# Float32 gathers from the residual, sums in other places, and a router without dependence on the group

## The chip, the cores and the metric

The kernel runs on one NeuronCore of a Trainium2 chip. The metric is the device time of one execution in microseconds, as the median of several runs. The engines are TensorE (PE; its weight loads are shown apart as PEld), VectorE (DVE), ScalarE (ACT), GpSimd (POOL) and SyncE (SP), whose queue issues nearly all the loads from HBM.

## The reference, cut to what matters

One decoder block on 256 tokens of width 2048, all in float32: two token mixers side by side, an output projection with a residual add, and a mixture of 32 experts. The change concerns the residual add and what follows it.

```python
x = x + mixed @ w_out[l]
x = x + hierarchical_moe(rms_norm(x, norm_ffn_g[l]), ...)
return rms_norm(x, norm_final_g)

def hierarchical_moe(h, ...):           # 4 groups of 8 experts, d_expert = 512
    group_prob = softmax(ht @ wr_group + br_group)
    g_prob, g_idx = top_k(group_prob, 1)
    expert_logits = (ht @ wr_expert + br_expert).reshape(n_tok, 4, 8)
    sel = expert_logits[arange(n_tok), g_idx[:, 0]]
    top_logit, top_idx = top_k(sel, 2)
    weights = softmax(top_logit) * g_prob
    gates = sum(one_hot(g_idx * 8 + top_idx, 32) * weights[..., None], axis=1)
    for e in range(32):
        hid = silu(ht @ w_gate[e]) * (ht @ w_up[e])
        out = out + gates[:, e:e + 1] * (hid @ w_down[e])
```

## The kernel before

**Dense part** (0 to about 798 us). The input projection, both mixers and their output projections run in an order that a list scheduler in the kernel works out at build time. Weights come as halves of 512 KB (`wr`, line 333, on SyncE's queue); ScalarE casts a half to `wh`, VectorE subtracts to get `wl`, and three matmuls (hi x hi, hi x lo, lo x hi) stand for one float32 product. The last step there makes the merged branches `mix` (16 steps j, four buffers). Then a loop written by hand does the output projection: four blocks n of 512 columns, eight steps kh each, and behind each block `after(n, pss)`: VectorE adds the block to the residual `acc`, ScalarE sums squares, TensorE transposes, ScalarE copies to `xT`, TensorE adds the router's logits into `pl`, and `xn` gets the block's split into a high and a low part (the function `split`: a cast on ScalarE, a subtraction on VectorE). The residual x is loaded into `acc` (line 1236) and the router's weights into `rt` (line 1244) from GpSimd's queue.

**Buffers.** Everything large lives in slots of [128, 2048] float32 (8 KB a partition) handed out by `slot(name)`; `room(n)` says whether n are left, `free(n)` gives back n. The `Experts` object `xw` streams the experts' weights: 384 tiles of 1 MB in one fixed order, for each expert eight gate/up tiles (`mgu`), and with one expert's delay four down tiles (`md`). A tile goes into a slot (`wt`) or into one of NX = 4 buffers `wx` that exist only after the dense part's pools are closed. `xw.issue` issues as many as there is room for (line 301, SyncE's queue), `xw.done` gives the used buffer back and issues the next.

**Router and experts.** After block 3 the root of the mean square (`rr`) scales the logits (`lg`); `first_max` finds the group, then the best and second-best expert in it, on 16 elements a partition; `asg` marks the chosen experts, four matmuls with a triangular mask count the tokens (`pos`, one less than the count), and `weights()` makes the gates. `gather(b)` builds, for the eight experts of group b, the compact inputs `xg`: a one-hot `oh` from `pos`, and for each of eight steps (d2) matmuls with lhsT = a part of `xn` (high and low) and the one-hot as moving operand, then two scaled copies on ScalarE. `spread(q)` makes one-hots `ohr`, gates and the transposed one-hots `ogT` for four experts. In the loop over e, expert 0's gather runs a step at a time between its own gate/up matmuls (`gu`); for later groups the gather runs beside the experts before (`beside`). Each expert: eight gate/up steps, `hd` = silu(gate) x up (ScalarE, VectorE), transposes, four down steps of the expert before (`down`), and `scatter`, which adds into `acc` two half experts at a time. `store` normalises and writes the output.

The profile names nearly all engine operations by the helper's line 167, so that tiles tell them apart.

## Time and profile before

| what | us |
| --- | --- |
| median of 3 runs | 1789.11 (1785.33 to 1793.22) |
| the profiled execution | 1787.91 |
| its span, first to last instruction | 1786.14 |
| TensorE matmuls busy | 1451.9 (81%) |
| VectorE busy | 821.4 (46%) |
| ScalarE busy | 556.5 (31%) |
| read from HBM | 526.82 MB |

The span counts from the first to the last instruction; what lies around it is 1.8 us. A timeline row is a run of like instructions: start, length, engine, line, operation, out<-in, shape, count; in brackets the idle time before it and the instruction that ended it. In a row of windows PEclk is the clock that TensorE was granted (1.00 is 2.4 GHz, 0.50 is 1.2 GHz), and the DMA share is the mean over 16 engines.

### The profile page before, as it was taken

What the parts mean: (1) busy time and instruction counts of PE and PEld (TensorE: products, weight loads), DVE (VectorE), ACT (ScalarE), POOL (GpSimd) and SP (SyncE); (2) the same over time, 40 slices, a digit from 0 to 9 for tenths busy, and PEclk for the clock granted to TensorE, in tenths of its full rate; (3) what the DMA queues carried; (4) which work ended last, traced back from release to release, by engine and by line L of the source; (5) the groups of instructions that cost most, each with busy time, mean ns of one, the idle gap of its engine ahead of it and who ended that gap; (6) DMA issues with size and microseconds to landing.
All of it is one profiled execution on the core that took longest, in us unless ns stands there. A gap on an engine that the chain in (4) does not pass through costs nothing.

```text
span 1786.1 us, 29643 instructions
## 1 busy us (share of the span) xinstructions
PE 1451.9 (81%) x12604; PEld 960.8 (54%) x12604; DVE 821.4 (46%) x1241; ACT 556.5 (31%) x919; POOL 33.6 (2%) x64
## 2 busy tenths in 40 slices
PE   7999999999999999996767776667676776676673
PEld 6989998888988999874323222223121332221120
DVE  6999998889944567442212121212121212121213
ACT  6668556666555344442001000011000110000002
POOL 0000000000100000000000000000000000000000
PEclk9999999999999999997978777798877888777766
DMA  6554463334635478538999999999999999999993
GB/s 232 180 163 133 147 209 107 118 105 158 190 117 177 152 254 331 176 125 330 414 421 421 420 421 421 421 420 421 421 421 421 421 420 421 421 421 420 420 421 149
DMA packets 94953, 534.09 MB, mean 299 GB/s; under 512 B 10528, under 2 KB 10544, under 8 KB 45024
## 3 DMA queue, kind: packets, MB, share of 16 engines
q1 hardware_dynamic: 91792, 522.49, 74.5%
q0 software_dynamic: 3024, 9.64, 1.8%
q8 instruction: 102, 1.67, 0.4%
q14 instruction: 35, 0.29, 0.0%
HBM read 526.82 MB, written 5.28 MB: 298 GB/s over the span
## 4 chain that ended last, share of the span: by engine, by line
DMA 49%; PE 40%; DVE 5%; ACT 3%; issue 2%; SPq 0%; DVEq 0%; ACTq 0%
PE mm L167 23%; DMA wt<-in_mgu_dram 21%; DMA wt<-in_md_dram 12%; DMA wx<-in_mgu_dram 11%; PE s L167 7%; PE sd L167 6%; DMA wx<-in_md_dram 3%; PE gu L167 2%; DVE wl L167 2%; DVE vring L167 1%; PE tr L167 1%; ACT wh L167 1%; PE y L167 1%; DMA x<-in_x_dram 1%; ACT ring L167 1%
## 5 line engine op out<-in xcount | busy, mean ns | idle before, releaser
L167 PE MATMUL mm<-hT,wh 128*128 128x256 f32 x2144 | 397.4, 287 | 5.7 <-ACT sg L167 3.0
L167 PEld LDWEIGHTS mm<-hT,wh 128*128 128x128 f32 x2144 | 330.1, 189 | 21.2 <-issue 9.9
L167 PE MATMUL gu<-wt,xg 128*32 128x256 f32 x2896 | 236.8, 457 | 102.8 <-DMA wt<-in_mgu_dram 94.5
L167 DVE TENSOR_TENSOR wl<-wr,wh 128x1024 fp32r<-128x1024 f32 x213 | 259.1, 1217 | 123.2 <-ACT wh L167 121.4
L167 PE MATMUL mm<-hT,wl 128*128 128x256 f32 x1072 | 302.7, 282 | 0.9 <-DVE wl L167 0.9
L167 ACT CAST wh<-wr 128x1024 fp32r<-128x1024 f32 x213 | 222.2, 1043 | 236.3 <-PE mm L167 150.2
L167 PEld LDWEIGHTS gu<-wt,xg 128*32 128x32 f32 x2896 | 88.8, 125 | 223.6 <-DMA wt<-in_mgu_dram 143.0
L167 PEld LDWEIGHTS mm<-hT,wl 128*128 128x128 f32 x1072 | 202.8, 189 | 1.5 <-DVE wl L167 1.3
L167 DVE TENSOR_TENSOR acc<-acc,sc 128x1024 f32<-128x1024 f32 x128 | 150.5, 1217 | 93.2 <-PE sc L167 93.2
L167 DVE SCALAR_TENSOR_TENSOR hd<-gu,gs,hd 64x256 f32<-64x256 f32 x32 | 15.7, 491 | 320.1 <-ACT hd L167 269.0
L167 DVE SCALAR_TENSOR_TENSOR ys<-y,gs,ys 128x512 fp32r<-128x512 f32 x32 | 24.0, 751 | 272.0 <-ACT ys L167 272.0
L167 PE MATMUL gu<-wx,xg 128*32 128x256 f32 x1200 | 104.7, 482 | 45.6 <-DMA wx<-in_mgu_dram 45.0
L167 ACT ACTIVATE ys<-y,gs 128x512 fp32r<-128x512 f32 x32 | 22.0, 687 | 280.0 <-PE y L167 280.0
L167 ACT ACTIVATE hd<-gu,gs 64x256 f32<-64x256 f32 x32 | 15.0, 468 | 259.5 <-PE gu L167 259.1
L167 PEld LDWEIGHTS gu<-wx,xg 128*32 128x32 f32 x1200 | 37.9, 130 | 99.5 <-DMA wx<-in_mgu_dram 68.7
L167 PE MATMUL sc<-ys,ogT 32*128 32x512 f32 x512 | 55.5, 509 | 28.8 <-DVE acc L167 27.7
L167 ACT ACTIVATE xg<-tr,prm 128x256 f32<-128x256 f32 x64 | 26.9, 471 | 161.2 <-PE tr L167 145.2
L167 ACT CAST ogT<-tr 128x256 fp32r<-128x256 f32 x32 | 11.8, 373 | 160.8 <-PE tr L167 160.7
L167 PEld LDWEIGHTS sc<-ys,ogT 32*128 32x128 f32 x512 | 23.6, 213 | 63.6 <-issue 43.6
L167 PEld LDWEIGHTS tr<-oh,xn 128*128 128x128 f32 x256 | 36.0, 209 | 15.5 <-issue 14.4
L167 PE MATMUL tr<-oh,xn 128*128 128x256 f32 x256 | 42.9, 315 | 1.0 <-DVE oh L167 1.0
L167 DVE TENSOR_TENSOR vring<-s,ring 128x512 f32<-128x512 f32 x64 | 42.4, 683 | 0.1
(462 smaller groups left out, 2042.4 us busy)
## 6 DMA issues: line engine op xcount, KB each, us to landing
wt<-in_mgu_dram SPq DMA_DIRECT2D x181, 1024.0 KB, 19.8
wt<-in_md_dram SPq DMA_DIRECT2D x87, 1024.0 KB, 19.8
wx<-in_mgu_dram SPq DMA_DIRECT2D x75, 1024.0 KB, 19.8
wr<-in_win_dram SPq DMA_DIRECT2D x132, 512.0 KB, 3.6
wx<-in_md_dram SPq DMA_DIRECT2D x41, 1024.0 KB, 19.8
wr<-in_wglu_dram SPq DMA_DIRECT2D x32, 512.0 KB, 3.8
wr<-in_wout_dram SPq DMA_DIRECT2D x32, 512.0 KB, 4.3
wr<-in_wro_dram SPq DMA_DIRECT2D x16, 512.0 KB, 6.7
```

The lines of the kernel that those rows point to most:

```text
L167: return self._tl.do(Op(self._k, lambda: f(*a, **k), c, outs, ins, own, fn, name == "dma_start"))
```

## The change

It has several parts that go together.

- The residual is now called `res`, and the gathers read it directly: lhsT is a float32 part of `res` and the one-hot is float32, so that four float32 matmuls stand where eight matmuls on the split parts stood. The split `xn` and its four slots go.
- The sums `acc` are two other slots, filled from `res` by four copies on ScalarE at the end of expert 0.
- The four buffers of `mix` are cut by k and given back in parts during block 3 (two at kh = 3, one at 5, one at 7); tiles are issued during `mix` up to 8 (before 7) and in the output projection when there is room.
- The best and second-best expert are found for all four groups at once, beside the group's own choice; `pos` keeps its one, and the one-hots compare with 1 to CAP. The Sqrt and the Silu table are loaded early by activations on a constant. Six matmuls whose result nobody reads stand between the logits and the choice.
- The gather runs one step ahead of the gate/up matmuls; `spread(0)` is cut in three, and its transposes come after `hd`.
- The branch for a group with too many tokens (not run with these inputs) is adapted.

```diff
-    acc = [slot("acc").rearrange("p (i c) -> p i c", i=2) for _ in range(2)]
+    res = [slot("res").rearrange("p (i c) -> p i c", i=2) for _ in range(2)]
...
-    xn = [[slot("xn", F32R) for _ in range(2)] for _ in range(2)]
     rt = slot("rt")
...
+        if n == 3:
+            act.activation(cst[:, 5:6], cst[:, 0:1], AF.Sqrt)
         for i in range(2):
-            a = A(i, n * 512)
+            a = B(i, n * 512)
...
         for i in range(2):
-            act.copy(xT[i], pts[i])
+            if n == 3 and i == 0:
+                dve.tensor_copy(xT[i], pts[i])
+            else:
+                act.copy(xT[i], pts[i])
...
-        for i in range(2):
-            cs = slice(n * 512, (n + 1) * 512)
-            split(xn[i][0][:, cs], xn[i][1][:, cs], A(i, n * 512))
...
-            if kh % 3 == 2:
+            if kh % 3 == 2 and (n < 3 or kh < 3):
                 xw.issue(xw.n + 1)
...
+            if n == 3 and kh in (3, 5, 7):
+                free(2 if kh == 3 else 1)
+                if kh == 3:
+                    xw.issue(xw.n + 1)
...
-    free(4)
+    ps = psd()
+    for _ in range(6):
+        pe.matmul(ps[:, :T], lhsT=ident, rhs=iot, start=True, stop=True)
...
+    acc = [slot("acc").rearrange("p (i c) -> p i c", i=2) for _ in range(2)]
     xw.more = NX
...
+    dve.tensor_reduce(m1, l32, axis=AX.X, op=OP.max)
+    dve.tensor_reduce(gm, l4, axis=AX.X, op=OP.max)
+    dve.tensor_tensor(x1, l32, e8(m1), op=OP.is_lt)
+    dve.tensor_tensor(xg_, l4, bc(gm, 4), op=OP.is_lt)
...
-    dve.tensor_scalar(pos, pos, 1.0, None, op0=OP.subtract)
...
+        act.activation(cst[:, 5:6], cst[:, 0:1], AF.Silu)
...
-                    for x_ in range(2):
-                        pe.matmul(ps[:, dd * 256:(dd + 1) * 256], lhsT=xn[i][x_][:, d * 128:(d + 1) * 128],
-                                  rhs=oh[i].rearrange("p a b -> p (a b)"), start=(i + x_ == 0), stop=(i + x_ == 2))
+                    pe.matmul(ps[:, dd * 256:(dd + 1) * 256], lhsT=B(i, d * 128, 128),
+                              rhs=oh[i].rearrange("p a b -> p (a b)"), start=(i == 0), stop=(i == 1))
...
-    next(gq)
+    for _ in range(2):
+        next(gq)
     ov2 = weights()
+    sp0 = spread(0)
+    next(sp0)
...
-                    next(gq)
+                    next(gq, None)
...
-                for _ in gq:
-                    pass
-                for _ in spread(0):
-                    pass
+                next(sp0)
                 gq = beside(0)
...
             act.copy(hT_, hps[:, 0:128])
+            if e == 0:
+                for h in range(2):
+                    for i in range(2):
+                        act.copy(acc[h][:, i], res[h][:, i])
```

What stands on SyncE's queue at the end of the dense part, before (`wr` are the last halves of the output projection's weights, `wx` and `wt` tiles of experts):

```order
L333 DMA wr_8609<-in_wout_dram 128x2x512
L333 DMA wr_8637<-in_wout_dram 128x2x512
L301 DMA wx_8769<-in_mgu_dram 128x2048
L301 DMA wx_8771<-in_mgu_dram 128x2048
L301 DMA wx_8773<-in_mgu_dram 128x2048
L301 DMA wx_8775<-in_mgu_dram 128x2048
L301 DMA wt_8777<-in_mgu_dram 128x2048
L301 DMA wt_8779<-in_mgu_dram 128x2048
L301 DMA wt_8781<-in_mgu_dram 128x2048
L301 DMA wt_8890<-in_mgu_dram 128x2048
L301 DMA wt_8911<-in_mgu_dram 128x2048
```

And after:

```order
L333 DMA wr_8607<-in_wout_dram 128x2x512
L333 DMA wr_8635<-in_wout_dram 128x2x512
L301 DMA wt_8655<-in_mgu_dram 128x2048
L301 DMA wx_8771<-in_mgu_dram 128x2048
L301 DMA wx_8773<-in_mgu_dram 128x2048
L301 DMA wx_8775<-in_mgu_dram 128x2048
L301 DMA wx_8777<-in_mgu_dram 128x2048
L301 DMA wt_8888<-in_md_dram 128x2048
L301 DMA wt_8905<-in_md_dram 128x2048
L301 DMA wt_8922<-in_md_dram 128x2048
L301 DMA wt_8939<-in_md_dram 128x2048
```

Before, seven tiles stand ahead of the first `wx`; after, twelve, the last of them behind the last half of the weights, and the four down tiles of expert 0 follow the `wx` directly. The first issue that waits for a tile of expert 1 is number 22 of the tiles before and number 24 after (counted from 0).

TensorE at the first gather, before (`tr` is the gather's result, `gu` the gate/up product of expert 0, `oh` the one-hots):

```order
L167 MATMUL tr_8871<-oh_686_8843,xn_8068 128x256
L167 MATMUL tr_8871<-oh_686_8843,xn_8069 128x256
L167 MATMUL tr_8871<-oh_687_8844,xn_8070 128x256
L167 MATMUL tr_8871<-oh_687_8844,xn_8071 128x256
L167 MATMUL gu_8870<-wt_7497,xg_8841 32x256 x8
L167 MATMUL tr_8892<-oh_686_8843,xn_8068 128x256
L167 MATMUL tr_8892<-oh_686_8843,xn_8069 128x256
```

And after:

```order
L167 MATMUL tr_8833<-oh_682_8829,res_8068 128x256
L167 MATMUL tr_8833<-oh_683_8830,res_8068 128x256
L167 MATMUL tr_8873<-oh_682_8829,res_8068 128x256
L167 MATMUL tr_8873<-oh_683_8830,res_8068 128x256
L167 MATMUL tr_8873<-oh_682_8829,res_8068 128x256
L167 MATMUL tr_8873<-oh_683_8830,res_8068 128x256
L167 MATMUL gu_8872<-wt_7499,xg_8827 32x256 x8
L167 MATMUL tr_8890<-oh_682_8829,res_8068 128x256
```

The second gather (`tr_8873`) now stands ahead of the first gate/up matmuls, the moving operand is the same one-hot, and the weights come from `res` instead of the two parts of `xn`.

ScalarE from the last block to the first gather, before (`rr` is the root, `ro_ge` and `ro_e` exponentials of the router):

```order
L167 ACTIVATE rt_8072,ssp<-acc_8065 128x512 x2
L167 COPY rt_8072<-sd_8729 128x512
L167 COPY rt_8072<-sd_8734 128x512
L167 ACT_TABLE_LOAD
L167 ACTIVATE rr<-rr,cst 128x2
L167 CAST xn_8068<-acc_8065 128x512
L167 CAST xn_8070<-acc_8065 128x512
L167 ACT_TABLE_LOAD
L167 ACTIVATE ro_ge_8794<-ro_ge_8794 128x8
L167 ACTIVATE ro_e_676_8821<-ro_e_676_8821 128x2
L167 CAST identr_8838<-ident 128x128
L167 ACTIVATE xg_8841<-tr_8871,prm 128x256 x2
```

And after:

```order
L167 ACT_TABLE_LOAD
L167 ACTIVATE cst<-cst 128x1
L167 ACTIVATE rt_8072,ssp<-res_8069 128x512 x2
L167 COPY rt_8072<-sd_8731 128x512
L167 ACTIVATE rr<-rr,cst 128x2
L167 ACT_TABLE_LOAD
L167 ACTIVATE ro_ge_8804<-ro_ge_8804 128x8
L167 CAST identr_8824<-ident 128x128
L167 ACTIVATE xg_8827<-tr_8833,prm 128x256 x2
L167 ACTIVATE ro_e_686_8841<-ro_e_686_8841 128x2
L167 ACT_TABLE_LOAD
L167 ACTIVATE cst<-cst 128x1
```

The first table load now stands ahead of the last block's squares, one of the two copies to `rt` and the two casts to `xn` are gone, and a third table load stands after the first gather's copies. Further down, `hd` of expert 0 stands directly behind the last `xg`; before, four casts to `ogT` and a table load stood between.

## Rows read from the trace of the kernel before

**Rows 1.** Windows: stretch, length, busy time (count) of each engine, PEclk, DMA share, GB/s.

```profile
690.00:798.00 108.00, 108.00 (x549) 90.97 (x548) 55.22 (x63) 47.19 (x64) 0.00 (x0) 1.00 0.52 172
...
804.00:818.00 14.00, 7.48 (x38) 5.51 (x38) 8.34 (x44) 2.09 (x7) 0.55 (x1) 0.51 1.01 424
...
842.00:846.00 4.00, 3.03 (x30) 1.54 (x34) 1.78 (x3) 0.66 (x2) 0.00 (x0) 0.50 0.00 0
...
880.00:1757.00 877.00, 608.48 (x5516) 217.97 (x5516) 184.32 (x202) 70.86 (x165) 1.01 (x2) 0.78 1.01 418
```

**Rows 2.** Chain of waits, start and length in us, the pieces that are tile transfers.

```profile
859.55 20.37 DMA wt<-in_mgu_dram
...
1727.72 19.82 DMA wx<-in_md_dram
```

**Rows 3.** Timeline of SyncE's queue: start, length, engine, line, operation, out<-in, count.

```profile
845.37 3.74 SPq L301 DMA_DIRECT2D wx<-in_mgu_dram  x3
```

**Rows 4.** Timeline of TensorE's matmuls, 808 to 844 us; idle time before in brackets.

```profile
808.54 0.61 PE L167 MATMUL tr<-ro_asg,mask 128*128 128x32 f32 x2 [6.31 <-DVE ro_asg L167]
...
811.01 2.07 PE L167 MATMUL tr<-oh,xn 128*128 128x256 f32 x8 [1.01 <-DVE oh L167]
814.00 1.94 PE L167 MATMUL gu<-wt,xg 128*32 128x256 f32 x16 [0.92 <-ACT xg L167]
...
819.51 1.21 PE L167 MATMUL tr<-oh,xn 128*128 128x256 f32 x8
821.28 1.07 PE L167 MATMUL gu<-wt,xg 128*32 128x256 f32 x16 [0.56 <-ACT xg L167]
...
836.15 1.95 PE L167 MATMUL tr<-ro_gtr,ohr 128*128 128x2 f32 x16
837.96 2.24 PE L167 MATMUL tr<-identr,ohr 128*128 128x128 f32 x8
...
843.38 5.34 PE L167 MATMUL gu<-wx,xg 128*32 128x256 f32 x48
```

**Rows 5.** Timeline of ScalarE, 800 to 842 us.

```profile
800.71 1.28 ACT L167 ACT_TABLE_LOAD   x1
802.00 0.30 ACT L167 ACTIVATE rr<-rr,cst 128x2 f32<-128x2 f32 x1
...
840.63 1.28 ACT L167 ACT_TABLE_LOAD   x1
```

**Rows 6.** Timeline of VectorE, 802 to 811 us.

```profile
802.93 1.28 DVE L167 TENSOR_TENSOR xn<-acc,xn 128x512 fp32r<-128x512 f32 x2
804.13 0.15 DVE L167 TENSOR_REDUCE ro_gm<-lg 128x2 f32<-128x8 f32 x1
...
805.38 0.27 DVE L167 TENSOR_REDUCE ro_sel<-ro_selp 128x16 f32<-128x64 f32 x1
...
808.17 0.22 DVE L167 TENSOR_TENSOR ro_asg<-ro_ohs,ro_go 128x64 f32<-128x64 f32 x1
...
810.30 0.20 DVE L167 TENSOR_SCALAR ro_pos<-ro_pos 128x64 f32<-128x64 f32 x1
```

**Rows 7.** Timeline of TensorE, two places with float32 matmuls of 256 columns.

```profile
195.13 1.10 PE L167 MATMUL sd<-SA,rkb 128*128 128x256 f32 x4 [0.21 <-ACT sg L167]
195.88 0.59 PE L167 MATMUL mm<-hT,wh 128*128 128x256 f32 x2
...
356.05 1.32 PE L167 MATMUL sd<-xg,gu 128*128 128x256 f32 x4
357.31 0.50 PE L167 MATMUL mm<-hT,wh 128*128 128x256 f32 x2
```

**Rows 8.** Weight loads of two tiles, duration min/median/max in ns.

```profile
L167 PEld LDWEIGHTS sd<-SA,rkb x4: 186/190/190, 195.1 to 195.6; 128*128 128x128 f32 x4
...
L167 PEld LDWEIGHTS tr<-oh,xn x192: 186/188/338, 921.6 to 1458.0; 128*128 128x128 f32 x192
```

**Rows 9.** DMA issues, 640 to 870 us: form, queue, count, KB, median us to landing.

```profile
rt<-in_rw_dram POOLq DMA_DIRECT2D x1, 288.0 KB, 12.7
```

More of the change, by code (lines that the diff above doesn't have):

```diff
@@ L411, in hybrid_block @@
     pool.iota(iot, pattern=[[1, T]], base=0, channel_multiplier=0, allow_small_or_imprecise_dtypes=True)
+    io8 = cp.tile([128, 8, 8], F32, name="io8")
+    pool.iota(io8, pattern=[[0, 8], [1, 8]], base=0, channel_multiplier=0, allow_small_or_imprecise_dtypes=True)
     mask = cp.tile([128, 2, 128], F32, name="mask")
@@ L1179, in front @@
             yield "wait"
-        mh = [[slot("mix", F32R) for _ in range(2)] for _ in range(2)]
-        St["mix"] = lambda k: [t[k // 8][:, (k % 8) * T:(k % 8 + 1) * T] for t in mh]
+        mh = [slot("mix", F32R) for _ in range(4)]
+        St["mix"] = lambda k: [mh[k // 4][:, (k % 4 * 2 + x_) * T:(k % 4 * 2 + x_ + 1) * T] for x_ in range(2)]
         yk = [[t[:, k * T:(k + 1) * T] for t in Y] for k in range(8)]
@@ L1191, in front @@
             if j % 2:
-                ctl(lambda: xw.issue(min(xw.n + 1, 7)))
+                ctl(lambda: xw.issue(min(xw.n + 1, 8)))
             while out_[0] > 1:
@@ L1232, in hybrid_block, with B @@
     mix = St["mix"]
[L1234 removed]
+    res = [slot("res").rearrange("p (i c) -> p i c", i=2) for _ in range(2)]
     for h in range(2):
[L1236 removed]
+        nc.gpsimd.dma_start(res[h], x.rearrange("(i p) c -> p i c", i=2)[:, :, h * 1024:(h + 1) * 1024])
+    def B(i, c, w=512):
+        return res[c // 1024][:, i, c % 1024:c % 1024 + w]
     def A(i, c, w=512):
         return acc[c // 1024][:, i, c % 1024:c % 1024 + w]
[L1241 removed]
     rt = slot("rt")
@@ L1377, in weights @@
     def weights():
+        e4, e2 = R("e4", [4]), R("e2", [1])
+        dve.tensor_sub(e4, m2, m1)
+        dve.tensor_mul(e4, e4, goh)
+        dve.tensor_reduce(e2, e4, axis=AX.X, op=OP.add)
+        act.activation(e2, e2, AF.Exp)
+        act.activation(cst[:, 5:6], cst[:, 0:1], AF.Silu)
         gs = R("gs", [1])
@@ L1388, in weights @@
         dve.tensor_mul(w2, w1, e2)
-        dve.tensor_mul(oh1, oh1, bc(w1, 8))
-        dve.tensor_mul(oh2, oh2, bc(w2, 8))
+        o8 = lambda o: o.rearrange("p i g e -> p i (g e)")
+        dve.tensor_mul(o8(oh1), o8(oh1), bc(w1, 32))
+        dve.tensor_mul(o8(oh2), o8(oh2), bc(w2, 32))
         dve.tensor_add(oh1, oh1, oh2)
-        dve.tensor_mul(gts.rearrange("p i (g e) -> p i g e", g=4), bc(oh1[:, :, None, :], 4, 8), g48)
+        dve.tensor_mul(gts.rearrange("p i (g e) -> p i g e", g=4), oh1, e8(goh))
         dve.tensor_copy(gtr[:, :, :, 0], gts)
         dve.tensor_copy(gtr[:, :, :, 1], bc(rr, 32))
-        ovf = R("ovf", [32])
-        dve.scalar_tensor_tensor(ovf, pos, float(CAP), gts, op0=OP.is_ge, op1=OP.mult)
-        ov1 = R("ov1", [32])
-        dve.tensor_scalar(ov1, pos, float(CAP), None, op0=OP.is_ge)
+        ovf, ov1 = (x_.rearrange("p i g e -> p i (g e)") for x_ in (x1, x2))
+        dve.scalar_tensor_tensor(ovf, pos, float(CAP + 1), gts, op0=OP.is_ge, op1=OP.mult)
+        dve.tensor_scalar(ov1, pos, float(CAP + 1), None, op0=OP.is_ge)
         ov2 = stile([128, 1], "ov2", 1)
@@ L1415, in gather @@
         xg = [slot("xg") for _ in range(2)]
-        oh = [stile([128, 8, CAP], "oh%d" % i, 1, F32R) for i in range(2)]
+        oh = [stile([128, 8, CAP], "oh%d" % i, 1) for i in range(2)]
         for i in range(2):
             pb = pos[:, i, 8 * b:8 * b + 8][:, :, None].to_broadcast([128, 8, CAP])
-            dve.tensor_tensor(oh[i], iot[:, None, 0:CAP].to_broadcast([128, 8, CAP]), pb, op=OP.is_equal)
+            dve.tensor_tensor(oh[i], iot[:, None, 1:CAP + 1].to_broadcast([128, 8, CAP]), pb, op=OP.is_equal)
         G8[b] = xg
@@ L1605, in hybrid_block @@
             down(e - 1, hT_)
+        else:
+            for _ in sp0:
+                pass
         if e < NE:
@@ L1624, in hybrid_block @@
             for i in range(2):
-                for x_ in range(2):
-                    pe.matmul(ps[:, i * 128:(i + 1) * 128], lhsT=xn[i][x_].bitcast(F32)[:, d * 128:(d + 1) * 128],
-                              rhs=dg[:, i], start=(x_ == 0), stop=(x_ == 1))
+                pe.matmul(ps[:, i * 128:(i + 1) * 128], lhsT=B(i, d * 128, 128), rhs=dg[:, i], start=True, stop=True)
             act.activation(h2[d // 8][:, (d % 8) * 256:(d % 8 + 1) * 256], ps[:, :256], AF.Copy, scale=P("ffng", d))
```

52 lines of the change are left out of this document (23 added, 29 removed).

## The prediction

> **What bounds the kernel now.** I read the windows by stage first, then the chain of waits, then the queue that issues the loads, then TensorE around the start of the experts. From 880 to 1757 us the DMA engines are busy all the time at 418 GB/s while TensorE works 608 of 877 us [rows 1]: the expert stage is bound by the 384 tiles of 1 MB. The chain says the same: from 859.55 us on it consists of tile transfers of some 20 us, each released by one that landed [rows 2]. By the count of issues the tile issued at 859.55 is number 33 (from 0) and landed at 879.92; the one that landed at 1747.54 is number 379 [rows 2]. That is 867.62 us for 346 tiles, 2.51 us a tile, without a gap. So the end is fixed by when the unbroken stream begins and with which tile. Just before it there is a hole: between 842 and 846 nothing moves at all [rows 1]. At 845.37 tile 22 is issued, in the buffer that expert 1's first tile gave back [rows 3]; expert 1's matmuls had begun at 843.38 [rows 4]. Of the tiles, 7 are in before the end of the dense stage, and 22 (0 to 21) are in or under way without expert 1. So: **end = issue of the first tile that waits for expert 1, plus 2.51 us for each tile left, plus a tail that the diff doesn't touch.** Two things can move it: that tile's number, and expert 1's start. Loading earlier by itself is worth nothing, since the hole would only open sooner.
>
> **Two buffers more.** Before, two buffers hold the sums and four the split of x; after, two hold x and two the sums. Two tiles more fit, and the issue order shows the first that waits for expert 1 at number 24 instead of 22. 2 x 2.51 = **5.0 us gained**. The sums take their buffers only after the eighth gate/up tile of expert 0, so nothing in front of it waits for them. Their four copies of 128x1024 on ScalarE run beside expert 1's matmuls, with about 7 us until ScalarE's next use: nothing. If that cover is gone, they cost some 4 us once. The five tiles more that load in the dense stage cost nothing if the weights' stream keeps its pace (a rival, below).
>
> **Router.** Removed from the path: the square-root table, 1.28 us before the root at 802.00 [rows 5], now loaded under the last block. But the logits also wait for the router's matmuls; with one of the two copies moved to VectorE these end some 0.5 us earlier, so of 1.28 us I take 0.9. The last split of x, two subtractions of 1.28 us together, lies between the logits and the first maximum at 804.13 [rows 6]: its part there is 1.1 us. The choice itself takes 804.13 to 808.39 [rows 6]. After, 13 steps depend on each other, on 64 elements; the nearest row of that size in such a chain is 0.27 us [rows 6], 3.5 us, and five small ones in between at about 0.1 make 3.5 to 4.0; saved 0.3 to 0.7, I take 0.5. The subtraction of one goes: 0.26 [rows 6]. Sum 0.9 + 1.1 + 0.5 + 0.3 = **2.8 us** (2.3 to 3.2). The six dummy matmuls lie in the gap of 6.31 us in which TensorE waits for the choice [rows 4]; at the size of [rows 7] their twelve instructions take 2.3 to 3.8 us, so they delay nobody. The Trainium skill, page "ScalarE: Activation LUTs", section "What ACT_TABLE_LOAD costs", counts 2.66 us for every switch, load and drain; here the root starts 0.01 us after a load of 1.28 [rows 5], so no drain shows. By the page the two loads taken off the path would bring 2.8 us more, a time of 1775.9.
>
> **Expert 0.** From the first gather to the end of its eight steps it takes 836.15 - 811.01 = 25.1 us [rows 4]. In the regular part a step is 2.77: gather 1.21, 0.56 of waiting for ScalarE's xg, gate/up 1.0 [rows 4]. One step ahead, the wait of 0.56 goes. The gather becomes four float32 matmuls, which run as eight instructions. Of that kind two rows are there [rows 7]: four in 0.75 us, from 195.13 to the next start at 195.88, which makes 1.5 us for eight; and four in 1.26 us (356.05 to the next start), 2.5 us for eight. In the gather, as in the first, the next matmuls come straight behind, and the last of the four overlaps them; I take 1.73, nearer to the first. A step is 1.73 + 1.0 = 2.73, eight are 21.9, with a first fill 22.1: 3.0 us less. Against it stands the clock: it was 0.51 from 804 to 818 [rows 1], after TensorE had had little to do since 802, and the first gather and the first gate/up took 2.07 and 1.94 instead of 1.21 and 1.07 [rows 4]. Before, about 7 us of gathering passed until the clock was back. At the low level the step takes double, so it loses half of what passes: 0 to 4.4 us. The dummies shorten the idle time and gathering begins without the pause of 0.92 [rows 4], so I take 2.6 lost, net **0.4 us gained** (3.0 gained to 1.4 lost; with the first row's 1.5 a step, 1.8 more gained).
>
> **From expert 0 to expert 1.** 836.15 to 843.38 are 7.23 us [rows 4]. In them: 1.95 for the gates' small matmuls, 2.24 for the transposes of the one-hots [rows 4], ScalarE's four casts behind them, the Silu table at 840.63 for 1.28 [rows 5], ScalarE's and VectorE's hd of 0.5 each, then two transposes. After, the table is loaded during expert 0, and hd stands ahead of the casts, right after the gates; the transposes run beside it. 1.95 + 2.24 + 0.47 = 4.7; and since the casts now come behind hd, the last pair of transposes may wait for a buffer, up to 0.9. So 4.6 to 5.5, I take 5.0: **2.2 us gained** (1.7 to 2.6). What is late next there is TensorE itself.
>
> **Later gathers.** The other three gathers have 0.5 us more work in each of eight steps (1.73 against 1.21), 4 us in some 56. TensorE is idle 30% of the stage [rows 1], so it is hidden.
>
> **Sum.** 5.0 + 2.8 + 0.4 + 2.2 = 10.4 us; ends 5.0 + 2.3 - 1.4 + 1.7 = 7.6 and 5.0 + 3.2 + 3.0 + 1.8 + 2.6 = 15.6. The profiled execution (1787.91, span 1786.14) would become 1777.5. It lies 1.2 under the median of 1789.11, so the forecast is 1778.7.
>
> **Rivals.** *The clock stays high* (0.22): the dummies hold it through the choice. Then nothing is lost in expert 0: 13.0 gained, 1776.1. Against it: what remains of the gap is some 4 us, and the dummies leave up to 2 of it empty.
> *Float32 gathers at the upper row* (0.13): 2.52 a step, 6.3 us more in eight steps; 4.1 gained, 1785.0. For it: [rows 7]'s second row, against it the first. The Trainium skill, page "TensorE: Matmul & The Clock Gate", section "Weight-path perf modes — Fast Weight Load (FWL) and DoubleRow", says that the fast load of 128 weights is given only where the type is not FP32, which speaks for it. The two load rows show 190 ns for float32 and 188 for the split kind [rows 8], so the trace shows no such difference.
> *The dense stage stalls* (0.15): the order puts both 1 MB loads of x after the late mix steps and the router's weights behind the last branch matmul (near 701 us), and VectorE's scaling of these stands in its queue ahead of subtractions that TensorE needs; five more tiles share the queue with the weights. TensorE is never idle from 690 to 798 [rows 1], so every stall there counts in full. The router's weights took 12.7 us to land [rows 9]; landing at 713.7 they would hold the subtractions up, which TensorE needs near 709.4, and with 2 us of scaling and subtracting the stall is 6.3; if they land in 5 us it is nothing. Taking 4: 6.4 gained, 1782.7.
> *The clock stays low through expert 0* (0.05), **the slower side**: each step is 3.46 + 1.94 = 5.4, eight are 43.2 against 25.1, and 5.0 + 2.8 + 2.2 no longer cover the 18.1: 8.1 lost, 1797.2. It decides from an expert 0 of 35.1 us. Against it: the clock came back in 7 us of the same sort of work before.
> *It doesn't do what it says* (0.05): the two tiles more are not under way because something else fills the buffers; 5.4 gained, 1783.7.
>
> **How the numbers follow.** The forecast itself has 0.40, with 1775.3 to 1781.5 of its own. A measurement of this kernel can tell about 0.5%, 8.9 us, from no change, a bound at 1780.2. Above it lie the float32 rival, the stall, the missing buffers and a part of the forecast; below it, most of the forecast and the high clock. Faster: 0.22 + three quarters of 0.40 + a little of the stall = 0.56. Slower: the low clock and a long stall, 0.07. The rest, 0.37, is within. The range goes from the sum's upper end (1773.5, with the clock kept and the shorter gather) to the upper float32 row with a bit over, 1773 to 1786; what it leaves out is the low clock, a long stall and the scatter of a median.
>
> **What would show it.** Right: twelve tiles issued before the wx tiles; tile 24 issued near 840 and expert 1 starting near 838; the end of the dense stage still at 798.2; a gather step of four float32 matmuls near 1.7 us at full clock; 4.6 to 5.5 us between expert 0's last gate/up and expert 1's first; a DMA hole longer than before, from about 830 to 840; the last tiles 10 us earlier. Wrong: TensorE idle between 700 and 720 (the stall), clock near 0.5 up to 830 (slower side), a step of 2.5 at full clock, or a hole after expert 1 has begun, in which case the stream isn't unbroken and the two tiles don't count.

## The result

| | kernel before | changed kernel |
| --- | --- | --- |
| median of 7 runs, us | 1789.11 (1785.33 to 1795.61) | 1779.18 (1774.03 to 1781.03) |
| the profiled execution, us | 1787.91 | 1781.03 |
| its span, us | 1786.14 | 1779.26 |
| first wx issue, us from the start | 798.22 | 804.93 |
| from the first wx issue to the end of the span, us | 987.9 | 974.3 |

The ratio is 0.9931, with a 95% interval of 0.9916 to 0.9947: faster, by 9.5 to 15 us. The forecast was 1778.7. The first wx issue, the first of the four tiles that go into the wx buffers, marks the end of the dense part. The two spans differ by only 6.9 us, and the last two lines of the table say why: behind that mark 13.6 us were gained, ahead of it 6.7 were lost. These are two separate findings.

**What was lost lies in code that the change doesn't touch.** Windows of the changed kernel around 355 us (stretch, length, busy time and count of PE, PEld, DVE, ACT, POOL, then the granted clock, the DMA share and GB/s):

```profile
350.00:355.00 5.00, 4.62 (x49) 2.73 (x47) 3.25 (x4) 4.55 (x9) 0.00 (x0) 1.00 0.31 105
355.00:360.00 5.00, 4.89 (x19) 3.77 (x19) 2.71 (x7) 0.90 (x2) 0.00 (x0) 0.69 0.31 108
360.00:365.00 5.00, 5.00 (x17) 3.58 (x16) 2.47 (x5) 1.21 (x2) 0.00 (x0) 0.50 0.00 0
```

And three windows of the kernel before, at the same place of the program:

```profile
350.00:355.00 5.00, 4.86 (x51) 2.80 (x49) 3.25 (x4) 4.56 (x9) 0.00 (x0) 1.00 0.32 105
355.00:360.00 5.00, 4.64 (x23) 3.04 (x23) 3.89 (x10) 1.61 (x5) 0.00 (x0) 1.00 0.32 108
360.00:365.00 5.00, 5.00 (x30) 3.73 (x30) 3.96 (x8) 3.89 (x5) 0.00 (x0) 1.00 0.00 0
```

The clock (the third number from the end) is 0.50 in one and 1.00 in the other, and TensorE gets 17 matmuls through in five microseconds instead of 30. This code is the same in both kernels. In the records of the weights' stream the changed kernel is 0.6 us ahead at 350 us and 6.8 us behind at 374, and stays at 6.6 until the output projection begins. Not every execution falls into this: the seven times of the changed kernel lie at 1774.0 to 1775.6 (three) and 1779.2 to 1781.0 (four), and of the twelve profiled executions here that have no edit in that place (before, changed and ten of the experiments) three show the low clock near 357 us. All three are of the changed kernel or its variants, ten of the twelve; the two on the kernel before are too few to say whether it falls there as often. An experiment below goes after it.

**What was gained.** The same stretches as in [rows 1] for the changed kernel; the program is 6.7 us later here, so read 842 to 846 against 835 to 839 of the kernel before:

```profile
690.00:798.00 108.00, 108.00 (x577) 92.11 (x576) 55.50 (x65) 47.12 (x62) 1.14 (x2) 1.00 0.71 253
...
842.00:846.00 4.00, 3.96 (x32) 2.28 (x36) 1.29 (x2) 3.31 (x7) 0.00 (x0) 0.50 0.01 4
```

TensorE is busy for the whole of 690 to 798, so the stall that I feared in the dense part isn't there, though the loads carry 253 GB/s where they carried 172. The hole in the loads is there as before (0.01 of the DMA engines at 842 to 846); it begins sooner, since tile 23 has landed at 840.6. SyncE's queue (start, length, engine, line, operation, out<-in, count):

```profile
786.99 0.34 SPq L301 DMA_DIRECT2D wt<-in_mgu_dram  x1
804.93 1.99 SPq L301 DMA_DIRECT2D wx<-in_mgu_dram  x4
...
845.42 0.33 SPq L301 DMA_DIRECT2D wt<-in_mgu_dram  x1
```

The issue at 845.42 is tile 24, the first to wait for expert 1. Counted from the first wx issue this is 40.5 us, where [rows 3] has tile 22 at 47.2. TensorE around expert 0, to be read against [rows 4]:

```profile
808.31 2.84 PE L167 MATMUL sd<-iot,ident 128*128 128x256 f32 x12
812.42 0.38 PE L167 MATMUL tr<-ro_asg,mask 128*128 128x32 f32 x2 [1.28 <-DVE ro_asg L167]
...
814.02 5.41 PE L167 MATMUL tr<-oh,res 128*128 128x256 f32 x16 [0.77 <-DVE oh L167]
819.36 1.07 PE L167 MATMUL gu<-wt,xg 128*32 128x256 f32 x16
820.36 1.99 PE L167 MATMUL tr<-oh,res 128*128 128x256 f32 x8
822.28 1.07 PE L167 MATMUL gu<-wt,xg 128*32 128x256 f32 x16
...
838.77 1.95 PE L167 MATMUL tr<-ro_gtr,ohr 128*128 128x2 f32 x16
840.58 0.84 PE L167 MATMUL tr<-identr,ohr 128*128 128x128 f32 x4
841.87 1.11 PE L167 MATMUL tr<-identr,ohr 128*128 128x128 f32 x4 [0.46 <-ACT ogT L167]
843.02 0.47 PE L167 MATMUL tr<-ident,hd 64*128 64x64 f32 x2
843.43 3.20 PE L167 MATMUL gu<-wt,xg 128*32 128x256 f32 x26
```

The step is now 2.92 us (819.36 to 822.28) without any wait in it; before it was 2.77, of which 0.56 were a wait. From expert 0's last matmuls to expert 1's first there are 4.66 us instead of 7.23. VectorE in the router, against [rows 6]:

```profile
808.51 0.42 DVE L167 SCALAR_TENSOR_TENSOR lg<-sd,rr,rbt 128x36 f32<-128x36 f32 x2 [1.10 <-PE sd L167]
808.96 0.22 DVE L167 TENSOR_REDUCE ro_m<-lg 128x8 f32<-128x64 f32 x1
809.10 0.15 DVE L167 TENSOR_REDUCE ro_gm<-lg 128x2 f32<-128x8 f32 x1
809.22 0.22 DVE L167 TENSOR_TENSOR ro_x<-lg,ro_m 128x64 f32<-128x64 f32 x1
```

And the logits of the kernel before:

```profile
802.60 0.42 DVE L167 SCALAR_TENSOR_TENSOR lg<-sd,rr,rbt 128x36 f32<-128x36 f32 x2
```

The first maximum now follows the logits at once (808.96 after 808.51); before, the first one ([rows 6], 804.13) came 1.5 us after them, with the subtractions of xn between. The small operations of the group lie between the large ones: 0.26 us from one large one to the next, with the small one inside. The logits wait for TensorE (1.10) and no longer for the root.

### The profile page after: what moved, and what is told of

Same layout as the page of the kernel before. It is cut to its first block, busy times and chain, and to the rows that moved or that the text cites. A ratio compares the mean times of both kernels' runs of the same rounds, so it can differ in the third digit from the quotient of the medians.

```text
span 1779.3 us, 29654 instructions
## 1 busy us (share of the span) xinstructions
PE 1472.8 (83%) x12616; PEld 980.9 (55%) x12616; DVE 816.6 (46%) x1233; ACT 555.6 (31%) x916; POOL 33.8 (2%) x65
## 4 chain that ended last, share of the span: by engine, by line
DMA 49%; PE 39%; DVE 7%; ACT 2%; issue 1%; SPq 0%; POOL 0%; DVEq 0%; ACTq 0%
DMA wt<-in_mgu_dram 28%; PE mm L167 22%; DMA wt<-in_md_dram 12%; PE s L167 7%; PE sd L167 6%; DMA wx<-in_md_dram 5%; DMA wx<-in_mgu_dram 3%; DVE wl L167 2%; PE tr L167 2%; DVE vring L167 2%; PE gu L167 1%; PE y L167 1%; ACT wh L167 1%; DVE vb L167 1%; DVE ts L167 1%
## 5 line engine op out<-in xcount | busy, mean ns | idle before, releaser
L167 PEld LDWEIGHTS mm<-hT,wh 128*128 128x128 f32 x2144 | 333.7, 191 | 21.9 <-issue 10.5
L167 PE MATMUL gu<-wt,xg 128*32 128x256 f32 x3104 | 262.1, 472 | 95.2 <-DMA wt<-in_mgu_dram 90.6
L167 PEld LDWEIGHTS gu<-wt,xg 128*32 128x32 f32 x3104 | 98.3, 128 | 228.7 <-DMA wt<-in_mgu_dram 135.2
L167 PE MATMUL gu<-wx,xg 128*32 128x256 f32 x992 | 78.2, 443 | 35.9 <-DMA wx<-in_mgu_dram 35.2
L167 PE MATMUL sc<-ys,ogT 32*128 32x512 f32 x512 | 59.2, 539 | 26.8 <-DVE acc L167 25.7
L167 PEld LDWEIGHTS gu<-wx,xg 128*32 128x32 f32 x992 | 29.5, 121 | 77.1 <-DMA wx<-in_mgu_dram 51.8
L167 PE MATMUL tr<-oh,res 128*128 128x256 f32 x256 | 67.1, 408 | 0.8 <-DVE oh L167 0.8
L167 ACT CAST ogT<-tr 128x256 fp32r<-128x256 f32 x32 | 11.7, 373 | 159.7 <-PE tr L167 159.6
L167 PEld LDWEIGHTS tr<-oh,res 128*128 128x128 f32 x256 | 48.6, 200 | 20.8 <-issue 13.9
```

Of the source, the lines that this page charges most:

```text
L167: return self._tl.do(Op(self._k, lambda: f(*a, **k), c, outs, ins, own, fn, name == "dma_start"))
```

## The experiments

All kernels are read by the stretch from the first wx issue to the end of the span, which leaves the scatter of the dense part out. Each row is one profiled execution; only the median is of several. From the landing of tile 33 to that of tile 379 a tile takes 2.507 to 2.509 us in all fourteen, so these 346 tiles differ by 0.4 us. What scatters is the stretch behind the last tile's landing, 25.6 to 28.7 us, and in some executions the loads pause again between tiles 24 and 33, up to 2.4 us in all. So a difference of 1 us at the end is not one; the landing of tile 33, the last column, leaves out what scatters behind it.

| kernel | median us (runs) | first wx issue | expert 1 starts, after it | tile that waits for expert 1, issued | end, after first wx | tile 33 landed, after first wx |
| --- | --- | --- | --- | --- | --- | --- |
| before | 1789.11 (7) | 798.2 | 45.2 | 22 at 47.2 | 987.9 | 81.7 |
| changed | 1779.18 (7) | 804.9 | 38.5 | 24 at 40.5 | 974.3 | 69.9 |
| hold2 | 1778.35 (4) | 800.5 | 38.5 | 24 at 43.7 | 977.0 | 72.5 |
| hold2b | 1783.03 (10) | 802.1 | 38.5 | 22 at 40.5 | 980.1 | 74.8 |
| late | 1775.95 (5) | 799.6 | 38.5 | 24 at 40.5 | 974.2 | 71.0 |
| twice0 | 1789.35 (10) | 799.6 | 50.7 | 24 at 51.9 | 984.1 | 80.5 |
| ahead | 1781.71 (6) | 800.5 | 38.7 | 22 at 40.7 | 980.6 | 75.4 |
| gap | 1783.55 (7) | 806.8 | 40.8 | 24 at 42.8 | 975.3 | 71.9 |
| no_idle_mm | 1777.97 (6) | 802.1 | 39.5 | 24 at 41.5 | 974.6 | 70.0 |
| split0 | 1781.47 (5) | 799.5 | 32.7 | 24 at 34.7 | 975.6 | 71.0 |
| split0b | 1773.86 (5) | 806.0 | 32.7 | 24 at 33.9 | 973.6 | 68.3 |
| more_later | 1774.90 (4) | 799.8 | 38.5 | 24 at 40.5 | 974.1 | 70.1 |
| steady | 1776.35 (5) | 800.2 | 36.6 | 24 at 38.6 | 972.7 | 67.3 |
| split0b_steady | 1775.85 (5) | 801.6 | 32.5 | 24 at 34.5 | 972.2 | 68.1 |

### How many tiles can wait without expert 1

My theory was that the end is set by the number of the first tile that waits for expert 1 and by expert 1's start; the rival, that two buffers more only move loads about.

```diff
...
+    live[0] += 2
     xw.more = NX
```

> The changed kernel with two buffers taken out of use from the end of the dense part on (and so ten tiles instead of twelve ahead of it, for lack of room). From the issue of the first wx tile to the end of the span the changed kernel takes 974.3 us and the kernel before 987.9; expert 1 starts 38.5 us after that issue in the changed kernel and 45.2 before. Theory (the end follows from the number of the first tile that waits for expert 1): that tile is number 22 again instead of 24, expert 1 starts at 38.5 as in the changed kernel, and the end comes 2 x 2.51 = 5.0 us later, 979.3 us from the first wx issue; some 8 us faster than the kernel before. Rival (the gain is that of the router and expert 0 alone, and the buffers only move loads to another time): 974.3 unchanged.

This missed, because the edit didn't do what I meant. It only raised the kernel's own count of buffers in use, and no tile was made that holds two of them. Tile 24 still was the first to wait, but for expert 1's third step instead of its first (43.7 against 40.5), and the end came 2.6 us later. hold2b takes two real ones (both also hold the tiles issued early to ten):

```diff
...
+    hold = [slot("hold") for _ in range(2)]
+    for t in hold:
+        pool.memset(t[:, 0:8], 0.0)
     xw.more = NX
...
     while todo:
         back()
+    hs = stile([128, 2, 8], "hs", 1)
+    for i in range(2):
+        dve.tensor_copy(hs[:, i], hold[i][:, 0:8])
     store()
```

> The changed kernel with two real buffers taken out of use: two tiles are written at the end of the dense part and read once after the last expert, so that no load can take their place (and ten instead of twelve tiles are ahead of the end of the dense part, which the run with seven showed to be worth nothing). The buffer of tile 22 is now given back by expert 1's first gate/up step, as in the kernel before; in the changed kernel that is tile 24. Theory (two tiles at 2.51 us): expert 1 starts 38.5 us after the first wx issue as in the changed kernel, and the end is 5.0 us later than its 974.3, 979.3. Rival (the buffers only shift loads): 974.3.

SyncE's queue in it:

```profile
842.53 2.04 SPq L301 DMA_DIRECT2D wt<-in_mgu_dram  x2
```

And TensorE:

```profile
840.54 3.64 PE L167 MATMUL gu<-wt,xg 128*32 128x256 f32 x32
```

Expert 1 starts at the same distance from the first wx issue as in the changed kernel (38.5), its first step gives a buffer back 2 us later, and the tile issued there has number 22. Tile 33 lands 4.9 us later than in the changed kernel, where 5.0 were expected from 2 x 2.51. At the end it is 5.8, of which 1.2 lie behind the last tile. The term stands.

### Are early tiles worth anything

```diff
-                ctl(lambda: xw.issue(min(xw.n + 1, 8)))
+                ctl(lambda: xw.issue(min(xw.n + 1, 7)))
...
-            if kh % 3 == 2 and (n < 3 or kh < 3):
-                xw.issue(xw.n + 1)
...
-                if kh == 3:
-                    xw.issue(xw.n + 1)
```

> The changed kernel with seven tiles instead of twelve loaded ahead of the end of the dense part; the five others are issued right behind the wx tiles, and the number of buffers in use stays. Theory (early transfers only make the hole before expert 1 longer): from the first wx issue to the end 974.3 to 975.5 us, the hole of 5 us between tile 23 and tile 24 closes, and expert 1 starts at 38.5 as in the changed kernel. Rival (each tile that is loaded early is 2.51 us off the end): 5 x 2.51 = 12.5 us later, 986.8.

974.2 against 974.3: five tiles fewer ahead of the experts cost nothing at the end, and 1.1 us at tile 33. Windows of it (columns as above):

```profile
820.00:830.00 10.00, 10.00 (x90) 6.18 (x90) 0.00 (x0) 3.36 (x8) 0.00 (x0) 1.00 1.01 420
830.00:840.00 10.00, 9.51 (x86) 6.63 (x88) 1.95 (x4) 4.47 (x10) 0.00 (x0) 0.81 1.01 420
840.00:850.00 10.00, 10.00 (x134) 5.79 (x126) 0.17 (x1) 2.64 (x4) 0.00 (x0) 0.85 1.02 422
```

The hole is closed and the loads run at 420 GB/s right through expert 1's start. So now the loads themselves, from the first wx issue on, are the bound, and this second bound lies about 1 us behind that of expert 1's start. That matters below.

### Does expert 1's start carry through to the end

```diff
-                for i in range(2):
+                for i in (0, 1) * (2 if b == 0 else 1):
```

> The changed kernel with every gather of the first group done twice over (eight float32 matmuls a step instead of four, the same result). A step's four take 1.92 us at the full clock. Theory (expert 1's start sets the end, one to one): expert 0 takes 8 x 1.92 = 15.4 us more, 40.1 instead of 24.8, expert 1 starts 53.9 us after the first wx issue, and the end is 15.4 us later, 989.7 us after that issue; slower than the kernel before by 2. Rival (the hole in the loads or the slack of later experts takes some of it up): under 10 us later.

TensorE in it:

```profile
820.91 1.07 PE L167 MATMUL gu<-wt,xg 128*32 128x256 f32 x16
821.92 3.72 PE L167 MATMUL tr<-oh,res 128*128 128x256 f32 x16
825.57 1.07 PE L167 MATMUL gu<-wt,xg 128*32 128x256 f32 x16
```

Four more matmuls cost 4.65 - 2.92 = 1.73 us (means of six steps) and not 1.92. The other 0.19 of a step's 1.92 come once a step; I put them down to the change over from one kind of matmul to the other, which no run shows alone. And in this execution no low clock fell into expert 0. So expert 1 came 12.2 us later instead of 15.4, the waiting tile was issued 11.4 later, tile 33 landed 10.6 later, and the end came 9.8 later. By its number that is the rival's "under 10 us"; by its steps it is nearly one to one. Of the missing 1.6 us, 0.8 went between the waiting tile and tile 33, where the changed kernel pauses longer: its expert 1 begins at the low clock and gives tile 25 its buffer 1.7 us behind tile 24, here it is 0.9. Another 0.1 went up to the last tile, and 0.7 lie behind it.

### One step ahead, alone

On the kernel before:

```diff
     gq = gather(0)
-    next(gq)
+    for _ in range(2):
+        next(gq)
...
                 if e == 0:
-                    next(gq)
+                    next(gq, None)
```

> The kernel before with one part of the change alone: the gather of expert 0 runs one step ahead of the gate/up matmuls, still on the split parts. Theory (the wait of 0.56 us a step for xg is what this part removes): seven such waits and the first of 0.92 go, 4.8 us; expert 0 takes 20.3 instead of 25.1 us, and the end comes 4.8 us sooner, 983.1 us from the first wx issue against 987.9. Had it stood alone, the float32 gather would then cost the changed kernel some 5 us in expert 0. Rival (the two buffers of the gather's result or ScalarE's copies set the step): it stays at 2.77 us and the time at 987.9.

```profile
813.59 3.78 PE L167 MATMUL tr<-oh,xn 128*128 128x256 f32 x16 [1.00 <-DVE oh L167]
817.30 1.07 PE L167 MATMUL gu<-wt,xg 128*32 128x256 f32 x16
818.30 1.22 PE L167 MATMUL tr<-oh,xn 128*128 128x256 f32 x8
819.45 1.07 PE L167 MATMUL gu<-wt,xg 128*32 128x256 f32 x16
```

The step is 2.15 us; the wait is gone. Expert 0 takes 18.4 us instead of 25.1, 1.9 less than the theory said; in it the clock was low for 3.7 us, in the kernel before for 6.9. Expert 1 starts 6.5 us sooner, tile 33 lands 6.3 sooner and the end comes 7.3 sooner, where the theory had 4.8: more than half of what the whole change brought, with two lines. And it gives the price of the float32 gather: 24.75 in the changed kernel against 18.4 here.

### The order between expert 0 and expert 1

```diff
-        act.activation(cst[:, 5:6], cst[:, 0:1], AF.Silu)
...
-                next(sp0)
+                for _ in sp0:
+                    pass
                 gq = beside(0)
```

> The changed kernel with the order between expert 0 and expert 1 of the kernel before: the transposes and casts of the first one-hots stand ahead of hd, and the Silu table is loaded there. Theory: the 4.66 us between expert 0's last gate/up and expert 1's first become 7.2, expert 1 starts at 41.1 instead of 38.5 us after the first wx issue, and the end is 2.6 us later, 976.9 instead of 974.3. Rival (the hole in the loads takes it up): 974.3.

```profile
842.44 1.99 PE L167 MATMUL tr<-identr,ohr 128*128 128x128 f32 x8
847.20 0.47 PE L167 MATMUL tr<-ident,hd 64*128 64x64 f32 x2 [2.77 <-DVE hd L167]
847.60 4.68 PE L167 MATMUL gu<-wt,xg 128*32 128x256 f32 x60
```

In the kernel before that wait is:

```profile
842.97 0.47 PE L167 MATMUL tr<-ident,hd 64*128 64x64 f32 x2 [2.77 <-DVE hd L167]
```

The wait of 2.77 us for hd is back, and expert 1 and the waiting tile come 2.3 us later. Of these 2.0 are there when tile 33 lands, and only 1.0 at the end: 0.3 went up to the last tile and 0.7 behind it. One execution can't settle more than that.

### The six idle matmuls

```diff
-    ps = psd()
-    for _ in range(6):
-        pe.matmul(ps[:, :T], lhsT=ident, rhs=iot, start=True, stop=True)
```

> The changed kernel without the six matmuls whose result nobody reads. Theory (they keep the clock through the choice): the three counting matmuls run at half the clock, 0.6 us more until the first gather, and the low clock lasts further into it: the first steps take 3.8 instead of 1.92 us, expert 0 takes 27 to 28.5 instead of 24.8, and the end is 2.5 to 4.5 us later, 977 to 979 us from the first wx issue instead of 974.3. Rival (the clock falls and comes back as it would anyway): within 0.7 of 974.3.

```profile
809.58 0.61 PE L167 MATMUL tr<-ro_asg,mask 128*128 128x32 f32 x2 [3.95 <-DVE ro_asg L167]
...
811.82 5.74 PE L167 MATMUL tr<-oh,res 128*128 128x256 f32 x16 [0.78 <-DVE oh L167]
817.49 1.07 PE L167 MATMUL gu<-wt,xg 128*32 128x256 f32 x16
818.49 1.99 PE L167 MATMUL tr<-oh,res 128*128 128x256 f32 x8
```

The counting matmuls did run at the low clock, 0.61 instead of 0.38 for a pair, and the first gather came 0.6 us later. But the first two gathers took 5.74 against 5.41, and the clock was back for the third in both. Expert 1 started 1.0 us later, tile 33 landed 0.1 later and the end didn't move by what can be told: the theory's 2.5 to 4.5 missed. In the changed kernel's execution the idle matmuls held the clock through the choice and didn't keep it from falling in the first gather; in that of steady it didn't fall there either.

### The first gather on the split parts

This keeps everything but the float32 form for the first group. The split parts' four buffers then stay until that gather is done.

```diff
...
-                    pe.matmul(ps[:, dd * 256:(dd + 1) * 256], lhsT=B(i, d * 128, 128),
-                              rhs=oh[i].rearrange("p a b -> p (a b)"), start=(i == 0), stop=(i == 1))
+                    for x_ in range(2 if b == 0 else 0):
+                        pe.matmul(ps[:, dd * 256:(dd + 1) * 256], lhsT=xn[i][x_][:, d * 128:(d + 1) * 128],
+                                  rhs=oh[i].rearrange("p a b -> p (a b)"), start=(i + x_ == 0), stop=(i + x_ == 2))
+                    if b:
+                        pe.matmul(ps[:, dd * 256:(dd + 1) * 256], lhsT=B(i, d * 128, 128),
+                                  rhs=oh[i].rearrange("p a b -> p (a b)"), start=(i == 0), stop=(i == 1))
...
+    parts(3)
     ov2 = weights()
...
+                    if kt == 6:
+                        free(4)
+                        acc += [slot("acc").rearrange("p (i c) -> p i c", i=2) for _ in range(2)]
```

> The changed kernel, but with the first group's gather on the split parts as before (eight matmuls of 0.15 us a step instead of four float32 ones that take 1.92), and only the later gathers on float32. The split parts' four buffers are given back when that gather is done, and the sums take two of them; the last block's split is made after the one-hots; seven tiles are loaded ahead of the end of the dense part. Tile 24 still is the first that waits for expert 1. Theory (expert 1's start sets the end): a step of expert 0 is 2.2 instead of 2.92 us, expert 0 takes 18.4 to 19.5 instead of 24.8, expert 1 starts at 32.2 to 33.3 instead of 38.5, and the end is 5.2 to 6.3 us sooner, 968 to 969 us from the first wx issue; faster than both kernels. Rival (the late split or the loads, which now come later, set expert 0's steps): 973 or more.

Expert 0 took 19.3 us and expert 1 started at 32.7, as expected, and the end still came at 975.6. Windows of it:

```profile
815.00:825.00 10.00, 9.92 (x115) 6.43 (x116) 1.71 (x6) 4.48 (x12) 0.54 (x1) 1.00 1.02 422
825.00:835.00 10.00, 9.51 (x93) 6.50 (x96) 1.95 (x4) 5.33 (x11) 0.00 (x0) 0.78 1.01 419
835.00:845.00 10.00, 10.00 (x132) 5.91 (x128) 0.17 (x1) 1.93 (x4) 0.00 (x0) 0.88 1.01 419
```

There is no hole. Tile 24's buffer was free at 34.7, but the tile landed only at 48.6, behind the seventeen others issued since the first wx. Tile 33 lands at 71.0, the same as in late, though expert 1 started 5.8 us sooner than there: with a fast expert 0 the other bound, the loads themselves, takes over. So I gave it three early tiles:

```diff
                 free(2 if kh == 3 else 1)
+                if kh < 7:
+                    xw.issue(xw.n + (2 if kh == 3 else 1))
```

> The kernel with the first group's gather on the split parts, with ten tiles instead of seven ahead of the end of the dense part (two issued after kh = 3 of block 3 and one after kh = 5). With seven, the loads ran without a gap from the first wx tile on, tile 24 landed at 48.6 us though its buffer had been free since 34.7, and the end stayed at 975.6. Theory (with a fast expert 0 the loads themselves had become the bound, and there early tiles count): three tiles less to load after the first wx issue, tile 24 lands at 40 to 41.5 us and the end comes 7 to 8 us sooner than with seven, at 967.5 to 969 us from the first wx issue; faster than both kernels by 5 us or more. Rival (something else holds the stream back, the scatter or the later gathers): 974 or more again.

Missed again: 973.6. Its windows:

```profile
816.00:826.00 10.00, 8.88 (x82) 6.23 (x81) 5.26 (x22) 5.85 (x13) 0.54 (x1) 0.85 0.88 345
826.00:836.00 10.00, 10.00 (x121) 6.80 (x119) 0.00 (x0) 3.36 (x8) 0.00 (x0) 1.00 0.84 302
836.00:846.00 10.00, 9.35 (x98) 6.24 (x101) 2.02 (x5) 5.81 (x10) 0.00 (x0) 0.83 1.01 424
```

Now the loads pause sooner, at 816 to 836 (345 and 302 GB/s): the four buffers held by the split parts are missing there, tiles 15 to 19 have to wait for expert 0's own steps, and tiles 20 to 23 come all at once when the gather is done, each 2.5 us behind the last. Tile 24 landed at 45.6. In the changed kernel it landed at 45.4. So the float32 gather buys four buffers for its 5.5 us. Tile 33 lands 1.6 us sooner here than in the changed kernel, and in split0b_steady 0.8 later than in steady: near this point the two are worth the same, by what these executions can tell.

### The later gathers

```diff
-                for i in range(2):
+                for i in (0, 1) * (2 if b and dd else 1):
```

> The changed kernel with half of the matmuls of the gathers for groups 2, 3 and 4 done twice over (six float32 matmuls a step instead of four, the same result), 0.96 us more a step, 7.7 us of TensorE a group, 23 us in all. Theory (TensorE is idle 29% of the stage, and what it is late the loads don't notice): the end stays at 974.3 us from the first wx issue, within 1. Rival (in the stretches with a gather TensorE is the bound, and the float32 form already costs there): some 23 us later, or 5 and more.

Windows of the instructions on the one-hots alone (busy time and count of PE, PEld and DVE, then as above), first the changed kernel, then this one at the same place of the program:

```profile
880.00:1757.00 877.00, 49.73 (x192) 35.93 (x192) 2.26 (x6) 0.79 1.00 416
...
875.00:1752.00 877.00, 70.17 (x288) 53.94 (x288) 2.26 (x6) 0.81 1.00 416
```

The three gathers take 20.4 us more of TensorE, and the end stayed at 974.1, tile 33 at 70.1. TensorE has room for half as much gather again without the loads noticing. The float32 form itself added 18.3 us there (31.44 in the kernel before), so it costs nothing that shows in the later groups.

### The low clock in the dense part

```diff
         for b in B4:
             ps, pg = psd(), psd()
+            for _ in range(3 if b == 0 else 0):
+                pe.matmul(ps[:, :T], lhsT=ident, rhs=iot, start=True, stop=True)
             by_head(ps[:, :T], b, nrm)
```

> The changed kernel with three full-size matmuls on constants (result overwritten) ahead of the 8-row matmuls in each of the two head blocks of the dense part, near 355 and 600 us. In the profiled execution of the changed kernel the clock was at half from 357 to 374 us there, and the end of the dense part came 6.7 us later than in that of the kernel before, whose clock stayed high; in other executions of this code the low stretch was missing. Theory (that low stretch is what makes executions of one kernel differ by some 6 us): no low stretch near 357, the first wx issue at 799 to 802 us, and no group of times above 1779. Rival (the clock falls there for another reason, or the scatter of the times has another source): the low stretch or both groups of times stay.

```profile
352.44 1.93 PE L167 MATMUL s<-vring,CR 128*32 128x256 f32 x32
354.30 1.56 PE L167 MATMUL sd<-iot,ident 128*128 128x256 f32 x6
355.80 0.50 PE L167 MATMUL sd<-nr,hsel_t 8*128 8x256 f32 x2
```

```profile
355.00:360.00 5.00, 5.00 (x27) 3.36 (x25) 4.34 (x11) 1.65 (x3) 0.00 (x0) 1.00 0.30 108
360.00:365.00 5.00, 5.00 (x29) 3.58 (x28) 4.17 (x8) 4.85 (x7) 0.00 (x0) 1.00 0.00 0
```

The clock stays at 1.00 there. The five times lie within 1774.6 to 1777.8, and the five of split0b_steady, which has both edits, within 1772.9 to 1777.9: ten executions, and none at 1779 to 1783, where eight of the 21 executions of the changed kernel, late, split0b and more_later are. If the edit did nothing, none of ten would still come about in some 3 cases of 100, so this speaks for the theory and doesn't prove it. The first wx issues of the profiled executions of the kernels without these matmuls line up the same way: 798.2 with no low clock in the dense part behind its first 25 us, 799.5 to 800.5 with one of 3.4 us near 410, 802.1 with 6.8, 804.9 to 806.8 where it fell near 357 for 14 to 17 us.

> Both: the first group's gather on the split parts with ten tiles early, and the three matmuls on constants in the two head blocks. Theory: the end 967.5 to 969 us from the first wx issue and that issue at 799 to 802, a time of 1769 to 1773 with little scatter. Rival: as for each alone, 1775 or more.

972.2 from the first wx issue, where the theory had 967.5 to 969, and a median of 1775.85, where it had 1769 to 1773: it missed by 3 us here too, for the reason found with split0b. Against the kernel before, steady has a ratio of 0.9924 (0.9906 to 0.9942), split0b 0.9916 (0.9891 to 0.9941) and split0b_steady 0.9917 (0.9897 to 0.9937). These overlap the changed kernel's interval; none is a clear step beyond it, though the slower group of times is gone from steady.

## Why the prediction was right, and where it wasn't

**The bound.** Right. The end follows from the number of the tile that waits for expert 1 and from when it is issued: hold2b moves the one, twice0 the other. From before to changed two tiles (5.0) and 6.7 us of expert 1's start make 11.7, and tile 33 lands 11.8 us sooner. Without this the diff, most of which is about arithmetic, can't be priced. What the formula lacked is the second bound 1 us behind it, the loads since the first wx issue. It hardly matters to this change (late), but to the next one (split0).

**Two buffers.** 5.0 forecast, 4.9 measured at tile 33 and 5.8 at the end (hold2b). The four copies into the sums are hidden, as forecast: they take ScalarE 3.9 us, and it sits idle for 6.1 behind them.

**Early tiles worth nothing.** Right within 1 us (late). The hole was placed wrongly: it was to last from about 830 to 840, and it lasts from 840.6 to 845.4, since tiles 19 to 23 are issued one by one as expert 0's steps give their buffers back.

**Router.** 2.8 forecast, 3.7 measured (first gather 12.8 us after the first wx issue before, 9.1 after), past the upper end of 3.2. The terms ahead of the first maximum were 0.9 + 1.1 and measured 1.9. Two others were mis-sized: the choice took 3.3 us, since the group's five small operations cost nothing between the large ones (I had given them up to 0.5); and the three counting steps took 0.86 instead of 1.50 us, since the idle matmuls held the clock there (0.61 a pair without them, no_idle_mm). I had priced those only for the gather. The 3.7 itself is read from the two traces; no run has the router's part alone.

**Expert 0.** 0.4 forecast and 0.4 measured (25.15 to 24.75), but by luck: two errors cancel. A gather step costs 1.92 us, not 1.73: the matmuls are as priced (twice0's four extra ones cost 1.73), but nothing stood in the sum for the other 0.19. At the full clock expert 0 takes 23.1 us (steady), where the forecast had 22.1, so 1.0 too little. Against it the low clock took 1.7 us (24.75 less 23.1) and not 2.6; the 4.4 at which that loss was bounded stands on no row, and nothing near it came.

**From expert 0 to expert 1.** 2.2 forecast, 2.6 measured, at the upper end. Hd did move ahead of the casts, and one pair of transposes does wait for a buffer, 0.46 us of the 0.9 allowed.

**Later gathers.** 6.1 us more of TensorE in each, where 4 were forecast (18.3 in the three); hidden all the same (more_later).

**The dense part.** No stall, as forecast: the router's weights landed in 6.3 us, not 12.7, and TensorE was busy throughout. But the forecast compared whole executions, and there it missed: one has 17 us of low clock near 357 us and the other has none.

**The sum.** From the first wx issue on 13.6 were gained where 10.4 was forecast: 1.3 us more from expert 1's start (6.7 against 5.4), and 2.1 behind the last tile, a stretch that the diff doesn't touch and that differs by 3 us among the executions here; 0.2 went the other way in between. That the median moved by 9.9, so close to the forecast, is partly luck: of the changed kernel's seven times four lie in the higher group, and the ratio of all runs says 12.3.

**The rivals.** The high clock didn't come about in the changed kernel's execution; it did in that of steady. The float32 gathers at the upper row, the stall, the low clock through expert 0 and the unused buffers were all refuted by the trace.

By the Trainium skill, page "ScalarE: Activation LUTs", section "What ACT_TABLE_LOAD costs", a switch would take 2.66 us; here the three loads of the changed kernel take 1.28 each again, and behind the last the next activation starts 0.02 us later, so the measurement decides for 1.28.

## What to carry to other kernels

Where a stage is bound by a stream of loads, ask which load is the first that can't be issued without the new stage's own progress, and price every edit by that load's number and time; edits that only move loads ahead of it are worth nothing as long as that load is the bound. Then look for the bound that lies right behind, since a second edit may gain nothing for that reason. And compare executions stage by stage from a common mark before you explain a difference of totals: in the two profiled executions here half of the gain was hidden by a stretch of low clock in code that the change doesn't touch.

## What the runs showed of the hardware

- TensorE's clock fell from 2.4 to 1.2 GHz near 357 us of the changed kernel's execution, behind 32 narrow matmuls (128x32 weights, 1.93 us) and two 8-row ones with gaps of 0.2 and 0.3 us, in a stretch in which the engine was busy 9.51 of 10 us (350 to 360). The same instructions with the same gaps, busy 9.50 of 10 us, kept the clock in the kernel before. With three full-size float32 matmuls in that place it stayed up in the profiled executions of steady and split0b_steady. What decides was not tried.
- A float32 matmul of 256 columns in the full array runs as two instructions and takes 0.43 us (1.73 for four, twice0). Four of them in a gather step take 1.92 with the change over; the eight on the split parts, which they replace, take 1.15 (818.30 to 819.45 in ahead).
- In the router's chain of dependent VectorE operations on 64 elements a partition a step takes 0.26 us (808.96 to 812.05 in thirteen operations), and the independent small one between two of them adds nothing to that.
